# The products of each inner tile in written TensorE order, and another order of the out-projection's products, in two Strassen FFNs on one Trainium2 core

## The chip, the cores and the metric

The kernel runs on one core of one Trainium2 chip. The metric is the device time of one execution in microseconds. The number given for a kernel is the median of its runs. Besides, one execution is recorded by the profiler; its span, from the first to the last instruction, lies a little under its own time, and every row quoted here is of that one execution.

## The reference

The program is one inference step of a streaming encoder with one convolution layer and one attention layer, each followed by a SwiGLU feed-forward network (FFN). 640 tokens (128 of running streams, 512 of a new one) of width 1024 go through it in float32. The change touches the two FFNs alone:

```python
def swiglu_ffn(h, g, w_in, w_out):
    a, b = jnp.split(rms_norm(h, g) @ w_in, 2, axis=-1)
    return h + (jax.nn.silu(a) * b) @ w_out
...
FFN_HIDDEN = -(-8 * D_MODEL // (3 * 256)) * 256
...
    for l in range(DEPTH):
        ...
        h = swiglu_ffn(h, norm_ffn[l], w_ffn_in[l], w_ffn_out[l])
    return rms_norm(h, norm_final), jnp.stack(new_hist, axis=0), k, v
```

The hidden width is 2816, which is 22 tiles of 128.

## The kernel before, in words

**Arithmetic.** A float32 matmul is made of three: each operand is cut into a high part (ScalarE copies it to fp32r, L371) and a low part (VectorE subtracts the high one, L372), and TensorE multiplies high by high, low weights by high tokens, and high weights by low tokens. `put` and `cut` do the cutting, `product` (L432) the three matmuls for each of four blocks of 128 along the contraction: 12 matmuls of 128x320 to one product.

**The FFN.** `ffn` (L333) works through the 22 inner tiles. For each tile the in-projection gives the two halves (a and b) over the two halves of 320 tokens. The first three tiles (`std`, L462) are computed in eight plain block products. The next 19 (`seven`, L524) take a Strassen-like form with seven products of weight sums and token sums. The products are named X11, X21, XT2, XT1, XT3, XT4 and X22 after the token block that they read. X11, XT2, XT3 and XT4 add up in one PSUM tile (`pa`). ScalarE copies `pa` away at three points (`keep`, L451: t1 after X11, t2 after XT2, t3 after XT3), since the next product adds on top of it. A product that goes on in `pa` must wait for the copy ahead of it. X21 stands in a tile of its own (`pb`); XT1 and X22 share a third (`pe`). The last two products, XT4 and X22, are not issued with their tile: `seven` returns a function `after`, and the tile behind it calls this as `before(0)` (XT4) and `before(1)` (X22).

**Weights.** `w_seven` (L410) brings one tile's weights: one 1 MB transfer issued on SyncE's queue (L414) into one of two `raw` buffers, two of 256 KB on GpSimd's into a buffer `s1` that sums two of the blocks, three additions on VectorE (L422, L423, L425) and seven cuts into a ring of 11 slots. A `raw` buffer is free once its last cut has been made, and the next transfer into it is issued then.

**The out-projection.** Tiles come in chunks of six (the first chunk has the three plain ones and three of `seven`). After each chunk `out_chunk` (L555) multiplies its hidden tiles by the output weights, in the same seven-product form for four groups u of output tiles. Its order is the string `QORD` (L65): `52` is product 5 of group 2, a `'` means its first two contraction blocks and a `"` the third alone, so that the work on the first four tiles goes ahead of that on the last two. `a0` and `a1` are the two left-over products of the chunk's last tile. Each finished output product is added to `h` on VectorE (L580).

**What sets the order.** A scheduler places the instructions of the program on each engine by a simulated timeline. `high_priority` lets a piece ahead, `issue_after` and `behind` put a piece after a given instruction. In `out_chunk` each product is issued after the one ahead of it in `QORD`. In `seven` nothing but the data ties the products: the scheduler places their matmuls.

In FFN 0 the `seven` tiles run from 284 to 640 us, in FFN 1 from 1066 to 1421 us. The second repeats the first 782.10 us later almost row by row.

Of the kernel before, what the change touches and what calls it, by code (L numbers as in the profile page):

```python
# [60 lines left out]
NH = NT // 2  # L61
X11, X21, XT2, XT1, XT3, XT4, X22 = range(7)
NCH, CW = 3, 6
HIX = {X11: 0, X21: 1, XT1: 2, XT2: 3, XT3: 4, X22: 5, XT4: 6}
QORD = """50' a0 a1 10' 50" 10" 20 60' 30' 51' 51" 11' 60" 30" 11" 21 70 61 31 40 52 71 12 22 41 62 32 53 72  # L65
          13 23 42 63 33"""
BO = "a0 s0 a1 s1 b0 b1 t0 n0 p0 c0 d0 t1 n1 c1 d1"
BL = "a0 o2 s0 a1 o2 s1 q2 t0 q2 n0 b0 q2 b1 q2 c0 q2 d0 t1 q2 n1 o2 c1 o2 d1 p0 o2"
# [14 lines left out]
def tile_trunk(ctx, tc, xT, vecs, hist, w_pw1, w_pw2, w_in0, w_out0, w_os0, w_in1, w_out1, w_os1,  # L83
               w_kq, w_v, w_o, rel, kc, vc, y_out, convp_out, convs_out, k_out, v_out):
    nc = tc.nc
# [19 lines left out]
    def mmt(n=512):  # L105
        return mm.tile([P, n], F32, tag="mm", name=nm("mm"))
# [4 lines left out]
    h = cst.tile([P, KT, NT], F32, name="h", tag="h")  # L111
# [24 lines left out]
    @contextmanager  # L136
    def behind(*ins):
        with ExitStack() as st:
            for i in ins:
                st.enter_context(tc.issue_after(i))  # L140
            yield
# [191 lines left out]
    def ffn(l, w_in, w_out, w_os, tail, hf, lead=(), b0=None, last_sum=()):  # L333
# [28 lines left out]
        sub, add, mult = ALU.subtract, ALU.add, ALU.mult  # L362
# [47 lines left out]
        def w_seven(src, out=False, first=(), rest=()):  # L410
            n = src.shape[-1] // 4
            raw, ws = wraw(), {}
            s1 = wx.tile([P, 512], F32, tag="s1", name=nm("s1"))[:, :n]
            nc.sync.dma_start(raw[:, :4 * n], src)  # L414
            a12, a11, a21, a22 = (raw[:, n * i:n * i + n] for i in range(4))
            with tc.high_priority(offset=HP), behind(*ties()):
                nc.gpsimd.dma_start(s1, src[:, 2 * n:3 * n])  # L417
                nc.gpsimd.dma_start(s1, src[:, 3 * n:4 * n], accum_op=add)
                for x in ((XT1, X11, X21, XT2, X22, XT3, XT4) if out else
                          (X11, X21, XT2, XT1, XT3, XT4, X22)):  # L420
                    if x == XT2:
                        nc.vector.tensor_tensor(out=a21, in0=a11, in1=a21, op=add)  # L422
                        nc.vector.tensor_tensor(out=a11, in0=s1, in1=a11, op=add)  # L423
                    elif x == X22:
                        nc.vector.tensor_tensor(out=a12, in0=a12, in1=a11, op=add)  # L425
                    ws[x] = slot()
                    with behind(*(first if x == XT1 else rest)):
                        cut(*ws[x], {XT1: s1, X11: a11, X21: a12, XT2: a11, X22: a12, XT3: a21,
                                     XT4: a22}[x])
            return ws  # L430

        def product(pt, w, xs, first, ks=None):  # L432
            (hi, lo), o0 = w
            n = len(xs)
            for k in ks or range(n):
                xh, xl = xs[k]
                c = slice(o0 + k * P, o0 + k * P + P)
                for i, (wt, v) in enumerate(((hi[:, c], xh), (lo[:, c], xh), (hi[:, c], xl))):
                    last = nc.tensor.matmul(pt, wt, v, start=(first and k == i == 0),  # L439
                                            stop=(k == n - 1 and i == 2), skip_group_check=True)  # L440
            return last

        def xproduct(pt, w, x, first):
            return product(pt, w, [(XH[x][:, k, :], XL[x][:, k, :]) for k in range(4)], first)
# [3 lines left out]
        def keep(tag, pt):  # L448
            t = tp.tile([P, NH], F32, tag=tag, name=nm(tag))
            with tc.high_priority(offset=HP):  # L450
                keeps.append(nc.scalar.activation(out=t, in_=pt, func=AF.Copy).ins)  # L451
            return t

        def plus(t, pt):
            with tc.high_priority(offset=HP):
                nc.vector.tensor_tensor(out=t, in0=pt, in1=t, op=add)

        def silu(t, src):
            with tc.high_priority(offset=HP):
                nc.scalar.activation(out=t, in_=src, func=AF.Silu)  # L460
# [27 lines left out]
        def combined(HH, HL, kp, second, held, neg, early=None):  # L488
# [32 lines left out]
                        own(XT4, b21)  # L521
            return sink

        def seven(src, sink, before):  # L524
            ws = w_seven(src)
            pa, pb = mmt()[:, :NH], mmt()[:, :NH]
            xproduct(pa, ws[X11], X11, True)
            t1 = keep("t1", pa)
            before(0)
            xproduct(pb, ws[X21], X21, True)  # L530
            plus(t1, pb)
            silu(t1, t1)
            before(1)
            xproduct(pa, ws[XT2], XT2, False)
            t2 = keep("t2", pa)
            pe = mmt()[:, :NH]
            xproduct(pe, ws[XT1], XT1, True)
            xproduct(pa, ws[XT3], XT3, False)
            t3 = keep("t3", pa)
            plus(t3, pe)  # L540

            def after(i):
                if i == 0:
                    last = xproduct(pa, ws[XT4], XT4, False)
                    sink(0, t1, pa)
                else:
                    last = xproduct(pe, ws[X22], X22, False)
                    plus(t2, pe)
                    silu(t2, t2)
                    sink(1, t2, t3)  # L550
                return last

            return after

        def out_chunk(c, HH, HL, after):  # L555
            ws, pts = {}, {}
            prod = {5: ("e", XT1, True, 1, 1), 1: ("a", X11, True, 0, 0),
                    2: ("b", X21, True, 0, 0), 6: ("a", XT2, False, 1, 0),
                    3: ("e", X22, False, 1, 0), 7: ("a", XT3, False, 1, 1),
                    4: ("a", XT4, False, 0, 1)}  # L560

            def go(i, u, part):
                if u not in ws:
                    o = (4 * c + u) * 12 * P
                    ws[u] = w_seven(w_os[:, o:o + 12 * P], True,
                                    (keeps[2:3], keeps[-2:-1])[u] if c == 0 and u < 2 else (),
                                    keeps[-1:] if (c, u) == (0, 1) else ())
                b, x, first, half, row = prod[i]
                if first and part != '"':
                    pts[b, u] = mmt()[:, :NH]  # L570
                pt = pts[b, u]
                with tc.issue_after(last[0]) if last else nullcontext():
                    ins = product(pt, ws[u][x], list(zip(HH[x], HL[x])), first,
                                  {"": None, "'": (0, 1), '"': (2,)}[part])
                last[:] = [ins.ins]
                if part == "'":
                    return
                hv = h[:, 2 * u + row, half * NH:half * NH + NH]
                with tc.high_priority(offset=HP):
                    nc.vector.tensor_tensor(out=hv, in0=hv, in1=pt, op=sub if row else add)  # L580

            last = []
            for t in QORD.split():
                if t[0] == "a":
                    with tc.issue_after(last[0]):
                        last[:] = [after(int(t[1])).ins]
                else:
                    go(int(t[0]), int(t[1]), t[2:])
            return lambda i: go((7, 4)[i], 3, "")

        def stats(half):
# [77 lines left out]
        for c in range(NCH):  # L669
            for jj in range(NSTD if c == 0 else 0, CW):  # L670
                if jj % 2 == 0:
                    held = [None] * 3
                if jj == NSTD and c == 0:
                    held = helds[1]
                after = seven(w_in[CW * c + jj], combined(HH, HL, jj // 2, jj % 2, held, True),
                              after)
            after = out_chunk(c, HH, HL, after)
            HH, HL = {}, {}
        hids = [(two(2 * jj), two(2 * jj + 1)) for jj in range(FT - NCH * CW)]
        for jj, hid in enumerate(hids):  # L680
            after = seven(w_in[NCH * CW + jj], plain(hid), after)
# [420 lines left out]
    for _ in ffn(0, w_in0, w_out0, w_os0, GR, hf, last_sum=last_sum)[1]:  # L1102
        pass
# [314 lines left out]
    for p in range(NP):  # L1418
# [7 lines left out]
        ha, sa, pt, ps = {}, {}, {}, {}  # L1426
        for op in (BL if p == NP - 1 else BO).split():
            i = int(op[1])
# [34 lines left out]
    with tc.high_priority(offset=HP):  # L1463
        sqs = xp.tile([P, KT, 384], F32, tag="xl1", name=nm("sqs")).rearrange("p a n -> p (a n)")
        acc, r = sqs[:, KT * NH:(KT + 1) * NH], sqs[:, (KT + 1) * NH:(KT + 1) * NH + 8]
        for k in range(KT):
            sq = square(h[:, k, 0:NH], NH, "a", sqs[:, k * NH:(k + 1) * NH])
            if k:
                sq_end = nc.vector.tensor_tensor(out=acc, in0=acc if k > 1 else sqs[:, 0:NH],
                                                 in1=sq, op=ALU.add).ins  # L1470
# [16 lines left out]
    for i in range(SPREAD_AT, KT):  # L1487
        with tc.issue_after(end):
# [4 lines left out]

    hf = ExitStack()
    spare, products = ffn(1, w_in1, w_out1, w_os1, ((256, 384), (0, 256)), hf,
                                     [(split_end[0], i) for i in (adds[1], adds[3], adds[5], sq_end)] +
                                     [(eps_end,)] * 2,
# [73 lines left out]
    last = [next(products) for _ in range(KT)][-1:]  # L1571
# [116 lines left out]
```

## Time and profile before

| | |
|---|---|
| median of 3 runs | 1460.97 us |
| lowest and highest run | 1460.22 and 1462.96 us |
| the profiled execution's own time | 1461.67 us |
| its span | 1459.5 us |
| granted TensorE clock in it | 0.999 |
| TensorE busy | 1432.7 us, 98% of the span |
| VectorE busy | 1144.6 us, 78% |
| ScalarE busy | 758.5 us, 52% |
| GpSimd busy | 297.5 us, 20% |
| moved by DMA | 192.56 MB, 132 GB/s on average |

Times of rows are counted from the start of the span. In a row of the timeline stand the start, the duration, the engine, the line, the operation, output and inputs, and in brackets how long the engine was idle before it and what released it. The matmuls overlap each other, so a busy TensorE is not one that has nothing to wait for: the distance from one start to the next is what counts.

### The profile page before, as it was taken

To read this page: it belongs to the slowest core of one execution; us is meant where nothing else is said; L and a number is where in the kernel's file an instruction comes from. 1 tells how busy PE (TensorE), PEld (TensorE's weight loads), DVE (VectorE), ACT (ScalarE), POOL (GpSimd) and SP (SyncE) were. 2 spreads that over 40 slices of the span, in tenths; PEclk is the share of its full clock that TensorE was granted. 3 is DMA by queue.
4 is the path that set the end of the run, shared out by engine and by line. 5 is a ranking of instruction groups with operands and counts; after the bars stand their busy time and mean duration, and the time that the engine had idled before them with its cause. 6 is when DMAs were issued, how large, how long until landed. Compare 5 with 4: busy or idle time off the path is not lost. (4 is left out here: it accounts for less than half of the span.)

```text
span 1459.5 us, 28220 instructions
## 1 busy us (share of the span) xinstructions
PE 1432.7 (98%) x11022; PEld 1369.1 (94%) x11022; DVE 1144.6 (78%) x2520; ACT 758.5 (52%) x1628; POOL 297.5 (20%) x349
## 2 busy tenths in 40 slices
PE   9999999999999999999999999999999999999998
PEld 8998799999999999999987898878999999999998
DVE  6789867988888888756768668577889788879855
ACT  4666554654554554545564355443554464555443
POOL 5699130011111111013222121011001111111101
PEclk9999999999999999999999999999999999999999
DMA  7267434044534444425556554452134543534522
GB/s 243 74 182 187 121 87 145 14 134 150 138 103 140 141 104 121 116 87 194 181 163 214 179 190 159 140 197 72 39 82 128 151 134 89 175 101 106 162 62 72
DMA packets 66932, 192.56 MB, mean 132 GB/s; under 512 B 12144, under 2 KB 30320, under 8 KB 58480
## 3 DMA queue, kind: packets, MB, share of 16 engines
q1 hardware_dynamic: 52432, 160.58, 33.5%
q0 software_dynamic: 13504, 29.37, 10.0%
q8 instruction: 86, 1.41, 0.4%
q10 hardware_dynamic: 864, 0.83, 0.2%
q14 instruction: 46, 0.38, 0.1%
HBM read 179.14 MB, written 11.61 MB: 131 GB/s over the span
## 5 line engine op out<-in xcount | busy, mean ns | idle before, releaser
L439 PE MATMUL mm<-XH,whi 128*128 128x320 f32 x896 | 276.4, 310 | 4.6 <-ACT t L451 4.2
L439 PE MATMUL mm<-XH,wlo 128*128 128x320 f32 x896 | 276.1, 309 | 0.0
L439 PE MATMUL mm<-XL,whi 128*128 128x320 f32 x896 | 273.9, 309 | 0.0
L371 ACT ACTIVATE whi<-raw 128x512 fp32r<-128x512 f32 (+2 forms) x280 | 168.5, 613 | 134.7 <-PE mm L439 113.5
L372 DVE TENSOR_TENSOR wlo<-raw,whi 128x512 fp32r<-128x512 f32 (+2 forms) x280 | 184.3, 667 | 23.4 <-ACT whi L371 21.6
L199 PE MATMUL mm<-xh,whi 128*128 128x320 f32 (+2 forms) x640 | 200.2, 314 | 1.1 <-ACT whi L164 0.8
L200 PE MATMUL mm<-xh,wlo 128*128 128x320 f32 (+2 forms) x640 | 198.2, 311 | 0.0
L201 PE MATMUL mm<-xl,whi 128*128 128x320 f32 (+2 forms) x640 | 195.9, 311 | 0.4 <-DVE xl L189 0.4
L439 PE MATMUL mm<-hid,whi 128*128 128x320 f32 x732 | 171.8, 310 | 2.7 <-DVE h L580 2.7
L439 PEld LDWEIGHTS mm<-XH,whi 128*128 128x128 f32 x896 | 167.8, 188 | 7.0 <-ACT t L451 6.3
L439 PEld LDWEIGHTS mm<-XH,wlo 128*128 128x128 f32 x896 | 168.2, 188 | 0.0
L439 PEld LDWEIGHTS mm<-XL,whi 128*128 128x128 f32 x896 | 167.6, 188 | 0.0
L439 PEld LDWEIGHTS mm<-hid,whi 128*128 128x128 f32 x732 | 125.1, 188 | 4.3 <-DVE h L580 4.3
L199 PEld LDWEIGHTS mm<-xh,whi 128*128 128x128 f32 x640 | 120.5, 188 | 4.4 <-ACT xh L187 1.5
L201 PEld LDWEIGHTS mm<-xl,whi 128*128 128x128 f32 x640 | 119.7, 188 | 1.2 <-DVE xl L189 0.8
L200 PEld LDWEIGHTS mm<-xh,wlo 128*128 128x128 f32 x640 | 120.5, 189 | 0.2
L439 PE MATMUL mm<-hid,wlo 128*128 128x320 f32 x366 | 113.0, 309 | 0.0
L439 PE MATMUL mm<-XH,shi 128*128 128x320 f32 x344 | 106.0, 309 | 1.1 <-ACT t L451 1.1
L439 PE MATMUL mm<-XH,slo 128*128 128x320 f32 x344 | 106.0, 308 | 0.0
L439 PE MATMUL mm<-XL,shi 128*128 128x320 f32 x344 | 105.6, 308 | 0.0
L841 POOL TENSOR_TENSOR ca<-ca,cvt 128x512 f32<-128x512 f32 x60 | 91.9, 1531 | 17.8 <-ACT cvt L838 11.2
L417 POOL DMA_DIRECT2D s<-in_w_in x38 | 22.1, 582 | 355.7 <-DVE wlo L372 142.2
(275 smaller groups left out, 3372.7 us busy)
## 6 DMA issues: line engine op xcount, KB each, us to landing
raw<-in_w_in SPq DMA_DIRECT2D x38, 1024.0 KB
s<-in_w_in POOLq DMA_DIRECT2D x76, 256.0 KB, 4.2
raw<-in_w_os SPq DMA_DIRECT2D x24, 768.0 KB
cache<-in_ck SPq DMA_DIRECT2D x32, 512.0 KB
cache<-in_cv SPq DMA_DIRECT2D x32, 512.0 KB
raw<-in_w_pw SPq DMA_DIRECT2D x11, 1024.0 KB
s<-in_w_os POOLq DMA_DIRECT2D x48, 192.0 KB, 3.7
raw<-in_w_kq SPq DMA_DIRECT2D x8, 1024.0 KB
```

Of the source, the lines that this page charges most:

```text
L199: nc.tensor.matmul(ps, wh, xh, start=(first and i == 0), stop=False)
L200: nc.tensor.matmul(ps, wl, xh, start=False, stop=False)
L201: end = nc.tensor.matmul(ps, wh, xl, start=False, stop=(stop and i == last))
L371: put_end[1] = nc.scalar.activation(out=hi, in_=src, func=AF.Copy).ins
L372: put_end[0] = nc.vector.tensor_tensor(out=lo, in0=src, in1=hi.bitcast(F32), op=sub).ins
L417: nc.gpsimd.dma_start(s1, src[:, 2 * n:3 * n])
L439: last = nc.tensor.matmul(pt, wt, v, start=(first and k == i == 0), stop=(k == n - 1 and i == 2), skip_group_check=True)
L841: nc.gpsimd.tensor_tensor(out=acc, in0=acc, in1=pr, op=ALU.add)
```

## The change

`seven` gets a list `row` that holds the last matmul of the product that was issued last, and a helper `following` that issues each product behind it. So the seven products of a tile, with the two left over from the tile ahead in their written places, stand on TensorE one after the other: X11, XT4 of the tile ahead, X21, X22 of the tile ahead, XT2, XT1, XT3. `out_chunk` begins behind the same instruction. The name `row` for the sign of an output product becomes `low` there, and lines move by two behind L524 and by nine behind L564. `QORD` takes another order in its second third: `60"`, `30"` and `70` come earlier, `51"` and `11` (now in one piece) and `40` too.

```diff
-QORD = """50' a0 a1 10' 50" 10" 20 60' 30' 51' 51" 11' 60" 30" 11" 21 70 61 31 40 52 71 12 22 41 62 32 53 72
+QORD = """50' a0 a1 10' 50" 10" 20 60' 30' 51' 60" 30" 51" 70 11 21 40 61 31 52 71 12 22 41 62 32 53 72
           13 23 42 63 33"""
...
+        row = []
+
         def seven(src, sink, before):
             ws = w_seven(src)
             pa, pb = mmt()[:, :NH], mmt()[:, :NH]
-            xproduct(pa, ws[X11], X11, True)
+
+            def following(f, *args):
+                with behind(*row):
+                    last = f(*args)
+                if last is not None:
+                    row[:] = [last.ins]
+
+            following(xproduct, pa, ws[X11], X11, True)
             t1 = keep("t1", pa)
-            before(0)
-            xproduct(pb, ws[X21], X21, True)
+            following(before, 0)
+            following(xproduct, pb, ws[X21], X21, True)
             plus(t1, pb)
             silu(t1, t1)
-            before(1)
-            xproduct(pa, ws[XT2], XT2, False)
+            following(before, 1)
+            following(xproduct, pa, ws[XT2], XT2, False)
             t2 = keep("t2", pa)
             pe = mmt()[:, :NH]
-            xproduct(pe, ws[XT1], XT1, True)
-            xproduct(pa, ws[XT3], XT3, False)
+            following(xproduct, pe, ws[XT1], XT1, True)
+            following(xproduct, pa, ws[XT3], XT3, False)
             t3 = keep("t3", pa)
             plus(t3, pe)
...
-                hv = h[:, 2 * u + row, half * NH:half * NH + NH]
+                hv = h[:, 2 * u + low, half * NH:half * NH + NH]
                 with tc.high_priority(offset=HP):
-                    nc.vector.tensor_tensor(out=hv, in0=hv, in1=pt, op=sub if row else add)
+                    nc.vector.tensor_tensor(out=hv, in0=hv, in1=pt, op=sub if low else add)
+                return ins
 
-            last = []
+            last = row[:]
```

Only TensorE, ScalarE and VectorE get another order, and only in the parts of both FFNs from their first `seven` tile on. The numbers of instructions stay, but for a few that do no work.

**TensorE where `seven` begins in FFN 0** (from 284 us on in the trace before). In the names, `mm_399_3438` is `pa` and `mm_403_3482` is `pe` of the first `seven` tile, `mm_400_3439` its `pb`, and `mm_407_3532` is `pa` of the second tile. XH0 to XH3 are the high tokens of X11, X21, XT2 and XT1. Left out are matmuls that go on in the same product. Before:

```order
L439 MATMUL mm_399_3438<-XH0_317_2811,shi_325_2834 128x320 [waits Activation_49]
L439 MATMUL mm_400_3439<-XH1_319_2813,shi_327_2836 128x320 [waits Activation_49]
L439 MATMUL mm_400_3439<-XH1_319_2813,slo_328_2837 128x320 [waits DVE_49]
L439 MATMUL mm_403_3482<-XH3_307_2801,whi_321_2830 128x320 [waits DVE_49,Activation_49]
L439 MATMUL mm_407_3532<-XH0_317_2811,whi_323_2832 128x320 [waits Activation_49]
L439 MATMUL mm_399_3438<-XH0_317_2811,slo_326_2835 128x320 [waits DVE_49]
L439 MATMUL mm_408_3533<-XH1_319_2813,whi_323_2832 128x320 [waits DVE_49]
L439 MATMUL mm_399_3438<-XH2_309_2803,shi_329_2838 128x320 [waits Activation_49]
```

After:

```order
L439 MATMUL mm_399_3438<-XH0_317_2811,shi_325_2834 128x320 [waits Activation_49]
L439 MATMUL mm_399_3438<-XH0_317_2811,slo_326_2835 128x320 [waits DVE_49]
L439 MATMUL mm_400_3439<-XH1_319_2813,shi_327_2836 128x320 [waits Activation_49]
L439 MATMUL mm_399_3438<-XH2_309_2803,shi_329_2838 128x320 [waits Activation_49]
L439 MATMUL mm_399_3438<-XH2_309_2803,slo_330_2839 128x320 [waits DVE_49]
L439 MATMUL mm_403_3482<-XH3_307_2801,whi_321_2830 128x320
L439 MATMUL mm_399_3438<-XH4_311_2805,whi_321_2830 128x320 [waits Activation_49]
L439 MATMUL mm_407_3532<-XH0_317_2811,whi_323_2832 128x320
```

Before, XT2 (the first matmul with XH2) stands 60 matmuls behind the first one of X11, with the X11 and X21 products of the second tile ahead of it; now it stands 24 behind.

**ScalarE at the second `seven` tile of FFN 0** (297 to 302 us in the trace before). `t3_404_3507` is the first tile's keep t3, `t1_409_3546` the second tile's keep t1, and `raw_415_3647` the third tile's weights. Before:

```order
L451 ACTIVATE t2_402_3480<-mm_399_3438 128x320 [waits PE_49]
L371 ACTIVATE shi_329_2838<-raw_405_3510 128x512 [waits DVE_49,Activation_49]
L371 ACTIVATE hid_383_3331<-B00_354_2976 128x320 [waits DVE_49]
L451 ACTIVATE t1_409_3546<-mm_407_3532 128x320 [waits DVE_49]
L371 ACTIVATE hid_389_3345<-B01_366_3109 128x320 [waits DVE_49]
L451 ACTIVATE t3_404_3507<-mm_399_3438 128x320 [waits PE_49]
L371 ACTIVATE whi_323_2832<-s1_430_3781 128x384 [waits DMASW7_49]
L371 ACTIVATE hid_377_3272<-hid_343_2852 128x320 [waits DVE_49]
L460 ACTIVATE t1_409_3546<-t1_409_3546 128x320 [waits DVE_49]
L451 ACTIVATE t2_412_3617<-mm_407_3532 128x320 [waits PE_49]
L371 ACTIVATE whi_321_2830<-raw_415_3647 128x512 [waits DMAHW5_49]
```

After:

```order
L451 ACTIVATE t2_402_3480<-mm_399_3438 128x320 [waits PE_49]
L371 ACTIVATE shi_329_2838<-raw_405_3510 128x512 [waits Activation_49]
L371 ACTIVATE hid_389_3345<-B01_366_3109 128x320 [waits DVE_49]
L371 ACTIVATE hid_377_3272<-hid_343_2852 128x320 [waits DVE_49]
L371 ACTIVATE whi_321_2830<-raw_415_3647 128x512 [waits DMAHW5_49,PE_49]
L451 ACTIVATE t3_404_3507<-mm_399_3438 128x320 [waits PE_49]
L371 ACTIVATE whi_321_2830<-raw_415_3647 128x512
L451 ACTIVATE t1_409_3546<-mm_407_3532 128x320 [waits PE_49]
```

The keep t3 of the first tile has changed places with the first cut of the third tile's weights, which waits for a DMA.

**VectorE near the end of the first chunk's out-projection** (343 to 351 us in the trace before). `raw_461_4193` is the weight buffer of the next tile, `raw_456_4098` that of the last group of output weights; `mm_454_4046` is the PSUM tile of group 2 in which products 12, 62 and 72 add up; its addition to `h` must have read it before the next of them goes on. `mm_455_4057` is that of 22, and `mm_449` that of 11, 61, 71 and 41. Before:

```order
L580 TENSOR_TENSOR h_73<-h_73,mm_455_4057 128x320 [waits DVE_49,PE_49]
L372 TENSOR_TENSOR wlo_322_2831<-raw_456_4098,whi_321_2830 128x384 [waits Activation_49]
L372 TENSOR_TENSOR slo_330_2839<-raw_456_4098,shi_329_2838 128x384 [waits Activation_49]
L580 TENSOR_TENSOR h_73<-h_73,mm_449_3933 128x320 [waits PE_49]
L372 TENSOR_TENSOR slo_328_2837<-raw_456_4098,shi_327_2836 128x384 [waits Activation_49]
L422 TENSOR_TENSOR raw_461_4193<-raw_461_4193 128x512 [waits DMAHW2_49]
L580 TENSOR_TENSOR h_73<-h_73,mm_454_4046 128x320 [waits PE_49]
```

After:

```order
L589 TENSOR_TENSOR h_73<-h_73,mm_449_3951 128x320 [waits PE_49]
L372 TENSOR_TENSOR slo_326_2835<-raw_456_4098,shi_325_2834 128x384 [waits Activation_49]
L422 TENSOR_TENSOR raw_461_4193<-raw_461_4193 128x512 [waits DMAHW2_49]
L425 TENSOR_TENSOR raw_456_4098<-raw_456_4098 128x384 [waits DVE_49]
L589 TENSOR_TENSOR h_73<-h_73,mm_454_4046 128x320 [waits PE_49]
L372 TENSOR_TENSOR wlo_322_2831<-raw_456_4098,whi_321_2830 128x384 [waits Activation_49]
L589 TENSOR_TENSOR h_73<-h_73,mm_455_4057 128x320 [waits DVE_49,PE_49]
```

The addition that waits for the next tile's DMA (L422) has moved up ten rows, from behind the additions to `h` of products 12, 22 and 41 to ahead of them.

More of the change, by code (lines that the diff above doesn't have):

```diff
@@ L567, in go @@
                                     keeps[-1:] if (c, u) == (0, 1) else ())
-                b, x, first, half, row = prod[i]
+                b, x, first, half, low = prod[i]
                 if first and part != '"':
```

## Prediction

> **What bounds the kernel.** I read the busy shares first, then the waits of TensorE, then the places of those waits in the timeline.
>
> ```profile
> PE 1432.7 (98%) x11022; PEld 1369.1 (94%) x11022; DVE 1144.6 (78%) x2520; ACT 758.5 (52%) x1628; POOL 297.5 (20%) x349
> 355.00:430.00 75.00, 75.00 (x514) 75.00 (x513) 63.54 (x122) 43.16 (x88) 9.99 (x14) 1.00 0.44 121
> PE mm L439 <- ACT t L451: 5.3, 10, 1.0
> PE mm L439 <- DVE h L580: 5.2, 9, 1.0
> ```
>
> TensorE sets the end. In the middle of a chunk (second row: busy time and instructions of PE, weight loads, VectorE, ScalarE and GpSimd, then clock, DMA share and GB/s) VectorE has 63.54 of 75 us to do, so it can be late only after a burst. The two last rows are what TensorE waits for in the FFNs: ten times the copy of a sum (keep, L451), nine times the addition of an output product to h. So an order that waits nowhere can win 10.5 us of 1459.5, under 1%; one wait of 4 us takes back as much as four of those 1.0 us.
>
> **Gain: the keeps.** One of the ten, at 296 us:
>
> ```profile
> 296.24 0.31 PE L439 MATMUL mm<-XL,shi 128*128 128x320 f32 x1
> 296.59 0.44 ACT L451 ACTIVATE t<-mm 128x320 f32<-128x320 f32 x1 [4.85 <-PE mm L439]
> 297.08 0.41 PE L439 MATMUL mm<-XH,whi 128*128 128x320 f32 x1 [0.53 <-ACT t L451]
> 297.33 0.31 PE L439 MATMUL mm<-XH,wlo 128*128 128x320 f32 x1
> 301.73 0.31 PE L439 MATMUL mm<-XH,wlo 128*128 128x320 f32 x1
> ```
>
> From 297.33 to 301.73 lie 30 steps, so a matmul takes 4.40/30 = 0.147 us. From the last matmul of XT2 to the first of XT3 it is 0.84 us, as XT3 stands directly behind and waits for the copy: 0.69 us lost, and 0.10 more as the next start follows after 0.25 instead of 0.147. In the new order 12 matmuls of XT1, 1.76 us, lie between XT2 and XT3, and six of output product 5 or twelve of X11 between XT3 and XT4. The chain of 0.84 us fits in either, over an idle ScalarE. Eight of the ten waits go, some 0.8 us each: **-6.4 us**. The two at the FFNs' very ends stay, as XT4 there has only two matmuls of other work ahead of it. Bounds: 0 if ScalarE is always late by another step, -10.5 if all waits of both kinds went.
>
> **Cost A: the first tile of seven in each FFN.** The new order asks for XT2 after 24 matmuls, the old one after 60. Who makes the low weights of XT2?
>
> ```profile
> 284.07 0.45 PE L439 MATMUL mm<-XH,shi 128*128 128x320 f32 x2
> 289.73 0.68 DVE L425 TENSOR_TENSOR raw<-raw 128x512 f32<-128x512 f32 x1
> 290.33 0.68 DVE L372 TENSOR_TENSOR slo<-raw,shi 128x512 fp32r<-128x512 f32 x1
> 290.94 0.48 DVE L372 TENSOR_TENSOR hid<-B,hid 128x320 fp32r<-128x320 f32 x1
> 291.34 0.68 DVE L372 TENSOR_TENSOR slo<-raw,shi 128x512 fp32r<-128x512 f32 x1
> 1066.17 0.46 PE L439 MATMUL mm<-XH,shi 128*128 128x320 f32 x2
> 1073.42 0.68 DVE L372 TENSOR_TENSOR slo<-raw,shi 128x512 fp32r<-128x512 f32 x1
> 284.00:296.00 12.00, 12.00 (x84) 12.00 (x83) 11.43 (x23) 5.22 (x11) 2.93 (x4) 1.00 0.40 78
> ```
>
> The row at 291.34 writes XT2's low weights, done at 292.02. It is the 390th VectorE instruction in both orders, and VectorE works without a break up to it (11.43 of 12 us): it comes no sooner. TensorE now wants it with the 26th matmul from 284.07 on, at 284.07 + 25 x 0.1467 = 287.74. It waits 292.02 - 287.74 = 4.3 and 0.1 for the restart, **4.4 us**. In FFN 1: 1074.10 - 1069.84 = 4.3, also **4.4**. Before, products of the second tile filled this time; they are not lost, but they don't cover any longer. Below it could fall only if VectorE had less to do ahead of row 390, and the pieces that move there are one of each kind in for one out, 0.6 us: 3.7 to 5.0.
>
> **Cost B: the second tile.** XT4 of the first tile waits for keep t3. In the new ScalarE order that keep stands directly behind the first cut of the third tile's weights, which waits for a transfer.
>
> ```profile
> 293.55 0.68 DVE L372 TENSOR_TENSOR wlo<-raw,whi 128x512 fp32r<-128x512 f32 x1
> 294.25 0.33 SPq L414 DMA_DIRECT2D raw<-in_w_in  x1
> 299.14 0.44 ACT L451 ACTIVATE t<-mm 128x320 f32<-128x320 f32 x1 [0.55 <-PE mm L439]
> 301.74 2.19 ACT L371 ACTIVATE whi<-raw 128x512 fp32r<-128x512 f32 x4 [0.41 <-DMA raw<-in_w_in]
> 480.51 0.33 SPq L414 DMA_DIRECT2D raw<-in_w_in  x1
> 485.37 0.69 DVE L422 TENSOR_TENSOR raw<-raw 128x512 f32<-128x512 f32 x1 [0.50 <-DMA raw<-in_w_in]
> ```
>
> The transfer is issued when the raw buffer's last cut ends (293.55 + 0.68 = 294.23, row 294.25), and ScalarE takes it at 301.74, 7.5 us on. The keep (299.14) went ahead of it before. In the new order VectorE makes that last cut one instruction later (0.40), so the data land at about 302.1; the cut takes 0.53 (the four of the group 2.19) and the keep 0.44. XT4 can go on at 303.1. TensorE reaches it 72 matmuls behind 284.07 (X11, X21, XT2, XT1, XT3 and the second tile's X11) and A's 4.4 us late, at 284.07 + 10.56 + 4.4 = 299.0. It waits 4.1, with the restart **4.2 us** in each FFN. Lower bound: a transfer as short as the one at 480.51 (485.37 - 480.51 = 4.9 us) lands at 299.5 and costs 1.5. Queued behind the cut are also the next keep and the cuts of the third tile; the latter are wanted a tile later, some 10 us.
>
> **Cost D: the chunks' output products.** The old order lets the addition L422, which waits for the next tile's transfer, stand ahead of the addition to h for which product 72 waits:
>
> ```profile
> 451.71 0.46 PE L439 MATMUL mm<-hid,whi 128*128 128x320 f32 x2
> 458.31 0.46 PE L439 MATMUL mm<-hid,whi 128*128 128x320 f32 x2
> 462.42 0.69 DVE L422 TENSOR_TENSOR raw<-raw 128x512 f32<-128x512 f32 x1 [2.34 <-DMA raw<-in_w_in]
> 463.03 0.48 DVE L580 TENSOR_TENSOR h<-h,mm 128x320 f32<-128x320 f32 x1
> 463.56 0.41 PE L439 MATMUL mm<-hid,shi 128*128 128x320 f32 x1 [0.99 <-DVE h L580]
> 327.29 0.42 PE L439 MATMUL mm<-hid,shi 128*128 128x320 f32 x1 [0.57 <-DVE h L580]
> ```
>
> Now L422 and L425 stand ahead of 12's addition, so 62 waits for it, and 62 stands 27 matmuls (3.96 us) ahead of 72. The transfer can't come as much sooner: it is released by product 40 (its last matmul in the 451.71 row), which moves ahead by only 18 matmuls, 2.64 us, and by a VectorE queue shorter by 0.8. In the second chunk: landing 462.42 - 3.44 = 459.0, then 0.61, 0.47 and 0.48 for the two additions and that to h: 460.5, against 62 at 458.45 (second of the 458.31 pair): 2.1 us instead of 1.24 before. By the same working the first chunk gets 0.8 for 0.6. Taken over six chunks, 0.7 each: **+4 us** (0 if the transfer lands 2 us sooner, 12.6 if each is 2.1 us late with no old wait to set against it).
> Earlier in the chunk 60" now comes 9 matmuls (1.32 us) sooner and 70 only six behind it. The wait at 327.29 is of this kind: the low parts of the chunk's last hidden tile are late. I put **+2.4 us** for both FFNs, 0.4 a chunk; 0 if the cuts come sooner with the written order, 6 x 1.32 = 7.9 if all of the 1.32 us becomes a wait.
>
> **Sum.** 2 x 4.4 + 2 x 4.2 - 6.4 + 4 + 2.4 = +17.2 us. Against the profiled execution's own 1461.67 this is 1478.9. That lies 0.7 above the median of 1460.97, so I say **1478 us**.
>
> The waits of A and B are longer than any TensorE wait in the FFNs before (1.0), and matmuls were slow once, at the start of the program:
>
> ```profile
> 2.00:6.00 4.00, 4.00 (x20) 4.00 (x20) 1.07 (x3) 1.51 (x2) 0.49 (x2) 1.00 0.97 329
> 7.00:9.00 2.00, 2.00 (x19) 2.00 (x19) 1.90 (x5) 0.85 (x2) 0.00 (x0) 1.00 0.98 339
> ```
>
> The first row has 20 matmuls in 4 us, 200 ns each, the second 19 in 2, 105 ns, though the clock column reads 1.00 in both: TensorE begins at half speed for some 4 us.
>
> **Rivals.** (1) *The transfer of B lands before keep t3 is wanted, or the keep is held only shortly.* For it: landing took 4.9 us at 480.51. Against: it took 7.5 here in the same traffic. B falls to 1.5 or less, and with D halved: 1478 - 5.4 - 3.2 = 1469. (2) *TensorE falls to the half speed of its start after each of the four waits.* For it: the rows above. Against: it is shown only for the start of the program; no wait inside the FFNs before reaches beyond 1.0. With 4 us at half speed behind each wait, 2 us of work lost each: 4 x 2 = 8, so 1486. The Trainium skill, "TensorE: Matmul & The Clock Gate", section "Part 1: The HAM clock gate (the "warmup" mystery)", has the clock halved after about one idle window of 3.4 us, and says that the window runs freely. An estimate by that page: a wait of 4.3 us covers a whole window in about a quarter of cases ((4.3 - 3.4) / 3.4), which makes 2 us of the 8 and a time of 1480; no row here can show it. (3) *The delay is earned back.* While TensorE waits 8 us in each FFN, VectorE and the transfers run ahead, and the waits of D shrink away. Against: each transfer is released by TensorE's own progress (two raw buffers), so a lead is kept for two tiles at most. D 0, old waits on h of 5.2 gone: 1478 - 6.4 - 5.2 = 1466. (4) *Faster: the start isn't held by VectorE.* If the rows ahead of 390 close up by 4 us once TensorE frees their slots in another order, A is 0, B by its lower bound 1.5 each, and D 0: 1461 + 3 - 6.4 = 1458. It decides where A, B and D come to less than 6.4 us in all. Against: 11.43 busy of 12 us leaves 0.6 to close up, not 4. (5) *The order isn't the written one.* The listing of the instructions shows it is.
>
> **Chances.** Forecast 0.60; (1) 0.13; (2) 0.08; (3) 0.12; (4) with what lies between it and no change, 0.07. The likeliest case by its own bounds (A 3.7 to 5.0, B 3 to 5, D 2 to 12) goes from 1461 + 13.4 - 6.4 + 2 = 1470 to 1461 + 20 - 6.4 + 12 = 1487. With (1) and most of (3) below it, the range is **1465 to 1487**. No change that can be measured here is within 0.2%, 2.9 us; that takes A to D at 3.5 to 9.3 us in all, 0.03; faster by more 0.04; slower 0.93.
>
> **What would show it.** A: in the changed trace a wait of about 4.3 us on VectorE's slo at 288 and at 1070 with the wait's end at 292.0. B: a wait of about 4 us on the keep near 299, ScalarE's cut of raw directly ahead of it, idle on a DMA. Gain: no wait on L451 between products inside the chunks. D: waits on the addition to h at 62 and 60" in place of 72. The forecast is wrong if VectorE's row 390 ends much before 292, if the third tile's transfer lands before 299, or if the waits are there and the time isn't.

## The result, and the profile after

| | before | after |
|---|---|---|
| median | 1461.97 us (4 runs, 1460.22 to 1464.0) | 1483.41 us (4 runs, 1481.02 to 1486.89) |
| the profiled execution's own time | 1461.67 us | 1481.02 us |
| its span | 1459.5 us | 1478.9 us |
| granted TensorE clock in it | 0.999 | 0.997 |

The runs before are the three given ahead and one more. The changed kernel takes 1.0139 times as long, with a 95% interval of 1.0121 to 1.0156. The page's busy shares after:

```profile
PE 1438.2 (97%) x11022; PEld 1371.2 (93%) x11022; DVE 1148.0 (78%) x2520; ACT 758.9 (51%) x1628; POOL 297.3 (20%) x349
```

The view of TensorE's waits after (total, times, longest):

```profile
PE mm L439 <- ACT t L451: 7.9, 6, 2.3
PE mm L439 <- DVE h L589: 5.6, 9, 0.9
PE mm L439 <- DVE slo L372: 4.6, 2, 2.3
PE mm L439 <- ACT shi L371: 3.2, 2, 1.6
PE mm L439 <- DVE hid L372: 3.0, 6, 0.5
```

The number of instructions and the work of the other engines are as before. The waits of TensorE in the FFNs were 5.3 + 5.2 = 10.5 us and are now 24.3. The waits on keeps (L451) are fewer, but longer: 10 of at most 1.0 us have become 6 of at most 2.3. Three kinds are new: the low and the high part of a weight sum (slo, shi), twice each, and the low part of a hidden tile (hid), six times.

**The start of the seven-product tiles.** The timeline of TensorE and VectorE in FFN 0, after:

```profile
283.62 0.31 PE L439 MATMUL mm<-XH,shi 128*128 128x320 f32 x1
288.89 0.41 PE L439 MATMUL mm<-XH,shi 128*128 128x320 f32 x1 [1.60 <-ACT shi L371]
290.88 0.68 DVE L372 TENSOR_TENSOR slo<-raw,shi 128x512 fp32r<-128x512 f32 x1
291.62 0.63 PE L439 MATMUL mm<-XH,slo 128*128 128x320 f32 x1 [2.31 <-DVE slo L372]
292.05 0.47 PE L439 MATMUL mm<-XL,shi 128*128 128x320 f32 x1
292.32 0.47 PE L439 MATMUL mm<-XH,shi 128*128 128x320 f32 x1
294.45 0.40 PE L439 MATMUL mm<-XL,shi 128*128 128x320 f32 x1
```

Two stretches of the windows view there, TensorE alone (its busy time and matmuls, the granted clock, DMA share, GB/s):

```profile
291.60:294.60 3.00, 2.98 (x11) 0.50 0.72 101
295.00:298.00 3.00, 3.00 (x22) 1.00 0.84 230
```

XT2 begins at 288.89 instead of 287.14, since the copy of its high part is late too, and then waits for the low part, written from 290.88 to 291.56. Both waits together are 4.33 us. Behind them matmuls start 0.267 us apart (292.05, 292.32). The windows say why: 11 matmuls in 3 us at a granted clock of 0.50, against 22 at 1.00 right behind.

**The keep behind a transfer**, the timeline of ScalarE and TensorE at the second tile:

```profile
301.30 0.63 ACT L371 ACTIVATE whi<-raw 128x512 fp32r<-128x512 f32 x1 [4.74 <-DMA raw<-in_w_in]
301.83 0.42 ACT L451 ACTIVATE t<-mm 128x320 f32<-128x320 f32 x1
302.31 0.42 PE L439 MATMUL mm<-XH,whi 128*128 128x320 f32 x1 [2.18 <-ACT t L451]
```

The cut waits 4.74 us for its data, the keep stands behind it, and XT4 waits for the keep.

**The turn from one chunk to the next**, the timeline of VectorE and TensorE:

```profile
366.41 0.42 PE L439 MATMUL mm<-hid,whi 128*128 128x320 f32 x1 [0.44 <-DVE h L589]
369.24 0.69 DVE L422 TENSOR_TENSOR raw<-raw 128x512 f32<-128x512 f32 x1 [0.68 <-DMA raw<-in_w_in]
369.85 0.48 DVE L589 TENSOR_TENSOR h<-h,mm 128x320 f32<-128x320 f32 x1
370.38 0.41 PE L439 MATMUL mm<-hid,whi 128*128 128x320 f32 x1 [0.63 <-DVE h L589]
```

The row at 366.41 is product 73, that at 370.38 is 43: these are the two that `out_chunk` leaves to the next chunk's first tile. 43 waits for the addition to h of 73, and that stands on VectorE behind L422, which waits for a transfer.

**The low part of the last hidden tile**, in the same view:

```profile
335.81 0.88 DVE L372 TENSOR_TENSOR hid<-B,hid 128x320 fp32r<-128x320 f32 x2
336.35 0.41 PE L439 MATMUL mm<-hid,shi 128*128 128x320 f32 x1 [0.50 <-DVE hid L372]
```

This is product 60". It waits 0.66 us in each of the six chunks and costs 0.94 with two restarts and a further short wait at 70.

In the table below a wait counts as what the distance between two starts has over 0.147 us, with the slower restart behind it; that is some tenths more than the idle time in the rows.

| in the profiled execution | before | after | difference |
|---|---|---|---|
| XT2 of the first tile, waits | - | 4.33 + 4.32 | +8.7 |
| slow steps behind it | - | 1.45 + 1.60 | +3.0 |
| keep t3 of the first tile, ahead of XT4 | - | 2.45 + 2.57 | +5.0 |
| the eight keeps that the change aims at | 6.8 | - | -6.8 |
| other keeps (513.60, 527.73 and 1205.58) | - | 0.29 + 1.82 + 1.63 | +3.7 |
| 60" and what follows at 70 | | 5.6 | |
| 62, 73 and 43 at the turn | | 9.8 | |
| output products in all | 8.3 | 15.4 | +7.1 |
| sum | | | +20.7 |

The own times differ by 19.35; the seven-product tiles began 0.45 us earlier (283.62 against 284.07). Where the other 0.9 us went was not traced.

### The profile page after: what moved, and what is told of

The parts are those of the page before. It is cut to its first block, busy times and chain, and to the rows that moved or that the text cites. A ratio compares the mean times of both kernels' runs of the same rounds, so it can differ in the third digit from the quotient of the medians.

```text
span 1478.9 us, 28238 instructions
## 1 busy us (share of the span) xinstructions
PE 1438.2 (97%) x11022; PEld 1371.2 (93%) x11022; DVE 1148.0 (78%) x2520; ACT 758.9 (51%) x1628; POOL 297.3 (20%) x349
## 5 line engine op out<-in xcount | busy, mean ns | idle before, releaser
L422 DVE TENSOR_TENSOR raw<-raw 128x512 f32<-128x512 f32 (+1 forms) x62 | 39.7, 640 | 73.3 <-DMA raw<-in_w_in 59.0
```

## The experiments

**chain_only**: the change with the former QORD.

```diff
-QORD = """50' a0 a1 10' 50" 10" 20 60' 30' 51' 60" 30" 51" 70 11 21 40 61 31 52 71 12 22 41 62 32 53 72
+QORD = """50' a0 a1 10' 50" 10" 20 60' 30' 51' 51" 11' 60" 30" 11" 21 70 61 31 40 52 71 12 22 41 62 32 53 72
```

> The change with the former QORD put back, so the chain of products alone. In the trace of the change the chain's own waits are 11.7 us at the two first tiles of seven (XT2), 5.0 us at the two second tiles (keep t3), 3.7 us on two later keeps and 9.9 us at the chunks' turns (73 and 43), and six waits of 0.94 us on the low parts of the last hidden tile (product 60") belong to the new QORD. Theory: the chain carries nearly all of it, so 1478 to 1483 us, with the waits at XT2, keep t3, 73 and 43 in place and the six waits at 60" gone. Rival: the new QORD carries half or more of the loss: 1472 us or less.

Measured: 1472.31 us (1467.98 to 1477.47), 1.0068 of before [1.0046, 1.0091]. The theory missed, and the time all but met the rival's 1472: the chain alone carries just under half of the loss. (The next run shows that the new QORD doesn't carry the other half alone.) The profiled execution was the slowest of the six, 1477.47 us. In it the waits at XT2 were there unchanged (4.34 and 4.33 us), and those at 60" and the long ones at 73 and 43 were gone (at most 0.5 us was left). In their place 72 waited for its addition behind L422, as in the kernel before. Its waits, and the longest one in the timeline:

```profile
PE mm L439 <- DVE h L589: 6.6, 6, 2.2
PE mm L439 <- ACT t L451: 5.0, 6, 2.0
```

```profile
583.70 0.69 DVE L422 TENSOR_TENSOR raw<-raw 128x512 f32<-128x512 f32 x1 [3.54 <-DMA raw<-in_w_in]
584.31 0.48 DVE L589 TENSOR_TENSOR h<-h,mm 128x320 f32<-128x320 f32 x1
584.85 0.42 PE L439 MATMUL mm<-hid,whi 128*128 128x320 f32 x1 [2.19 <-DVE h L589]
```

**qord_only**: the kernel before with the new QORD alone (the same lines the other way round).

> The kernel before with the new QORD alone. Theory: the products of the in-projection stay where the scheduler put them, so no wait at XT2 of the first tile and none at 73 and 43; what comes is at most six waits of 0.94 us at 60", against 3 to 5 us of old waits that go: 1460 to 1466 us. Rival (the order of the output products moves the transfer behind which the additions to h queue): 1468 us or more.

Measured: 1460.14 us (1459.15 to 1463.21), 0.9985 [0.9974, 0.9995]. The theory held. In its waits those at 60" came (the first row), and others on h went from 5.2 to 2.5:

```profile
PE mm L439 <- DVE hid L372: 4.2, 6, 1.0
PE mm L439 <- ACT t L451: 2.6, 6, 0.5
PE mm L439 <- DVE h L580: 2.5, 5, 0.6
```

So the parts don't add up: +0.68% and -0.15% make +1.39% together. The new QORD wins a little where the scheduler may place 73 and 43 freely, and loses where the chain holds them in their written places. The next run tests the second half of this; the former QORD with 73 and 43 free was not run.

**free_turn**: the chain without 73 and 43. `tiles[0]`, here and below, counts the tiles of seven in an FFN from 1; tiles 4, 10 and 16 begin behind a chunk. The lines that do the counting are left out.

```diff
-            following(before, 0)
+            (following if tiles[0] not in (4, 10, 16) else lambda f, i: f(i))(before, 0)
...
-            following(before, 1)
+            (following if tiles[0] not in (4, 10, 16) else lambda f, i: f(i))(before, 1)
```

> The change, with the two left-over output products of each chunk (73 and 43) left out of the chain; the rest stays chained. Theory: in the changed kernel 73 stands nine matmuls behind 63 and 43 twelve behind 73, and their additions to h stand on VectorE behind cuts or behind L422, which waits for a transfer; with 24 and 18 matmuls between them the waits of 9.9 us over six chunks go: 1483.4 - 9.9 = 1473.5 us. Rival (VectorE is late there whatever stands between, so the next product waits instead): less than 3 us are won, 1480 us or more.

Measured: 1472.8 us (1471.96 to 1474.25), 1.0069 [1.0054, 1.0084]. The theory held: 10.6 us won. The waits at 73 were gone in all six chunks, those at 43 were 0.3 to 1.1 us in five. On TensorE 24 matmuls now stood between 63 and 73. That it equals the time of chain_only agrees with the place: either part of the change without the other leaves 73 and 43 all but free of waits.

**free_start**: the chain begins with the third tile.

```diff
-                with behind(*row):
+                with behind(*(row if tiles[0] > 2 else ())):
```

> The change, with the first two tiles of seven of each FFN left out of the chain (it begins with the third). Theory: the waits at XT2 (5.8 and 5.9 us with the slow matmuls behind them) and at the keep t3 ahead of XT4 (2.5 and 2.6) go, one wait of 0.8 us on a keep in each FFN comes back: 1483.4 - 16.8 + 1.6 = 1468 us, and every later wait stays. Rival (the delay is only moved: VectorE and the transfers lose the lead that the waits gave them): later waits grow and the time stays above 1475 us.

Measured: 1469.54 us (1467.47 to 1474.17), 1.0039 [1.0022, 1.0056]. By the medians the theory held within 1.5 us. In the timeline the start shows only the keep wait of the kernel before:

```profile
297.24 0.41 PE L439 MATMUL mm<-XH,whi 128*128 128x320 f32 x1 [0.53 <-ACT t L451]
```

But the later waits did not all stay as they were. In the profiled execution (1472.75 us, 3.2 above the median) the waits behind the first two tiles come to 26.9 us in both FFNs, against 20.2 in the changed kernel. Most of the 6.7 us is at product 10" of the first chunk, which waited 1.4 and 2.9 us for hidden low parts and in the changed kernel not at all. The longer one:

```profile
1111.15 0.56 DVE L422 TENSOR_TENSOR raw<-raw 128x384 f32<-128x384 f32 x1 [1.42 <-DMA raw<-in_w_os]
1112.09 0.49 DVE L372 TENSOR_TENSOR hid<-B,hid 128x320 fp32r<-128x320 f32 x1
1112.63 0.41 PE L439 MATMUL mm<-hid,whi 128*128 128x320 f32 x1 [2.64 <-DVE hid L372]
```

The low part stands on VectorE behind an addition that waits for output weights. In the changed kernel the same addition finds its data landed:

```profile
1118.86 0.56 DVE L422 TENSOR_TENSOR raw<-raw 128x384 f32<-128x384 f32 x1
```

So a part of the delay at the start is earned back later, as the rival says, though far less than the rival asks for.

**keep_ahead**: the third tile's cuts behind the first tile's keep t3.

```diff
-            ws = w_seven(src)
+            t3 = keeps[-4:-3] if tiles[0] == 3 else ()
+            ws = w_seven(src, False, t3, t3)
```

> The change, with the cuts of each FFN's third tile of seven put behind the keep t3 of its first tile, so that this keep doesn't stand behind a cut that waits for a transfer. Theory: the waits ahead of XT4 (2.5 and 2.6 us) go, the cuts lose 0.4 us of no account: 1483.4 - 5 = 1478.4 us, with the wait at XT2 unchanged. Rival (the tile is late for another reason, such as X21 of the second tile or the weights of the third): the wait reappears within a tile and the time stays within 1 us.

Measured: 1480.82 us (1477.65 to 1482.25), 1.0120 [1.0104, 1.0136]. In the timeline the keep no longer waits for the cut, and the cut still waits for its data:

```profile
299.04 0.44 ACT L451 ACTIVATE t<-mm 128x320 f32<-128x320 f32 x1 [1.84 <-PE mm L439]
301.93 1.15 ACT L371 ACTIVATE whi<-raw 128x512 fp32r<-128x512 f32 x2 [2.45 <-DMA raw<-in_w_in]
310.48 0.41 PE L439 MATMUL mm<-XH,shi 128*128 128x320 f32 x1 [0.92 <-ACT t L451]
```

XT4 went through, but the second tile's XT3 waited at 310.48, 1.2 us (0.4 in FFN 1). Of 5.0 us, 3.5 were won in the trace. The medians differ by 2.6, but the intervals of the two kernels overlap. The rows show the order on ScalarE as the cause of this wait, and that a part of it passed to the next keep.

**warm_gap** and **warm_gap24**: 12 or 24 wasted matmuls in each FFN's first tile between X21 and XT2. XT1 starts its tile anew, so nothing of them gets into the result.

```diff
             following(before, 1)
+            if tiles[0] == 1:
+                pe = mmt()[:, :NH]
+                following(xproduct, pe, ws[X11], X11, True)
+                following(xproduct, pe, ws[X21], X21, True)
             following(xproduct, pa, ws[XT2], XT2, False)
...
-            pe = mmt()[:, :NH]
+            if tiles[0] > 1:
+                pe = mmt()[:, :NH]
```

(warm_gap has the first of the two products alone.)

> The change, with 12 wasted matmuls (one more X11 product into the tile of XT1, which XT1 overwrites) in each FFN's first tile of seven between X21 and XT2, where TensorE waits 4.3 us. In the trace of the change the ten to twelve matmuls behind that wait start 0.267 us apart instead of 0.147. Theory: TensorE slows down because it stood still for over 4 us; with the 12 matmuls it stands still 2.6 us at a stretch, the matmuls behind come 0.147 us apart and the end of the wait doesn't move: 1.4 us less in each FFN, 1480.5 us. Rival (the slow steps have to do with the weights or with VectorE's writes at that time): they stay 0.267 us apart and the time doesn't change.

Measured: 1483.71 us (1482.0 to 1488.02), 1.0143 [1.0118, 1.0168]: no gain. Behind a wait now under 2 us, seven matmuls came 0.147 us apart, and then 13 came 0.26. The timeline, and windows of half a microsecond:

```profile
292.22 0.41 PE L439 MATMUL mm<-XH,slo 128*128 128x320 f32 x1 [1.70 <-DVE slo L372]
293.36 0.34 PE L439 MATMUL mm<-XL,shi 128*128 128x320 f32 x1
293.50 0.46 PE L439 MATMUL mm<-XH,shi 128*128 128x320 f32 x1
293.76 0.47 PE L439 MATMUL mm<-XH,slo 128*128 128x320 f32 x1
```

```profile
292.50:293.00 0.50, 0.50 (x5) 1.00 0.00 0
293.50:294.00 0.50, 0.50 (x4) 0.50 0.76 111
296.50:297.00 0.50, 0.50 (x4) 0.59 0.92 136
297.00:297.50 0.50, 0.50 (x5) 1.00 0.39 98
```

In FFN 1 the same wait was followed by no slow steps. The clock fell from 293.50 on for 3.4 us, though TensorE had been busy again for 1.3 us. That no time was won has a further reason: XT4's waits for the keep were still there, 2.36 us at 303.11 and 3.40 at 1093.42, and slow steps now stood behind both. The FFNs had four such stretches of 3.4 us in this execution, against two in the changed kernel. Neither the theory (a wait of over 4 us is needed) nor its rival says that; the last section takes it up.

> As warm_gap, with 24 wasted matmuls (products X11 and X21 into the tile that XT1 overwrites) in place of 12, so that TensorE stands still for under 1 us of the 4.3. With 12, still standing 2 us, it was slow behind one of the two waits (14 steps of 0.267 us) and not behind the other (2). Theory (the slow steps come from standing still): in both FFNs the matmuls behind XT2's first two come 0.147 us apart, and the end of XT2's wait stays where it was: 1.2 to 2.9 us less in each FFN, 1479 to 1481 us. Rival (they come from something else at that place): 10 or more slow steps in at least one FFN.

Measured: 1476.09 us (1472.79 to 1478.81), 1.0095 [1.0073, 1.0117]. With TensorE busy throughout there were no slow steps at this place in either FFN, as the theory said. It was 3 us faster than expected. One reason lies in the order: with the wasted matmuls in its timeline the scheduler put keep t3 ahead of the cut of raw again, and the wait ahead of XT4 was gone too. The slow steps had to do with standing still, then. The same kernel shows them at another place, behind a 1.9 us wait at 331.39.

**mid_chain**: free_start and free_turn together.

> The change, with both the first two tiles of seven and 73 and 43 left out of the chain. Theory: the two savings add up, since the waits lie in different places: free_start's 1469.5 less the 10.9 us that its trace shows at 73 and 43, 1459 us, a little under the kernel before. Rival (they share a cause, VectorE's backlog, and one replaces the other): 1464 us or more.

Measured: 1461.43 us (1457.93 to 1463.46, 10 runs), 0.9984 [0.9973, 0.9996]. The two savings add up nearly: 2.4 us are missing. Product 10" of the first chunk waited 2.1 and 1.8 us, which it does not in free_turn, and waits of 2.9 us stayed at 43, in five turns. With both places free, nothing is left of the loss, and nothing is won either: qord_only, without any chain, has the same ratio (0.9985).

**qord_mid**: the kernel before, no chain, a third order.

```diff
+QORD = """50' a0 a1 10' 50" 10" 20 60' 30' 51' 11' 60" 30" 51" 70 11" 21 40 61 31 52 71 12 22 41 62 32 53 72
           13 23 42 63 33"""
```

> The kernel before with a third order of the output products: as the new QORD, but with the first part of 11 (six matmuls, 0.88 us) ahead of 60", and its last part behind 70. Theory: the six waits of 0.75 to 1.3 us on the low parts of the last hidden tile at 60" shrink by 0.7 us each: 1460.1 - 4 = 1456 us. Rival (the early sum of 11 takes a PSUM tile, or VectorE is late by more): 1460 us or more.

Measured: 1458.37 us (1456.69 to 1459.31), 0.9968 [0.9955, 0.9981]. The time lies between the theory's 1456 and the rival's 1460. It beats the kernel before, by 0.3%, and the changed one. The waits at 60" shrank to 0.4 us or none; the first chunks got one of 1.8 us at 40, which keeps back part of the gain.

**mid_both**: mid_chain with the order of qord_mid.

> mid_chain (the change without the chain in the first two tiles of seven and without 73 and 43 in it) with the order of output products of qord_mid. Theory: the two gains add up; mid_chain's six waits of 0.64 to 0.76 us at 60" and six of 0.2 behind it shrink by 0.5 us each, 3 us: 1461.4 - 3 = 1458 us, no better than qord_mid alone (1458.4), since the chain's remaining gain at the keeps (two waits of 0.8 in place of four) is given back at 10" of the first chunk (2.1 and 1.8 us). Rival (the chain in the middle of the chunks is worth what the keeps cost): 1455 us or less.

Measured: 1464.80 us (12 runs, 1462.36 to 1466.3), 1.0018 [1.0007, 1.0028]. Both readings fell: with the other QORD the chain cost 0.5% again (1.0018 against 0.9968). The trace shows four waits of 1.1 to 1.4 us and several shorter ones on keeps, in and near the turns. The first of the four, on VectorE, ScalarE and TensorE:

```profile
365.79 0.69 DVE L422 TENSOR_TENSOR raw<-raw 128x512 f32<-128x512 f32 x1 [1.76 <-DMA raw<-in_w_in]
368.12 0.47 ACT L460 ACTIVATE t<-t 128x320 f32<-128x320 f32 x1 [3.85 <-DVE t L456]
369.01 0.42 ACT L451 ACTIVATE t<-mm 128x320 f32<-128x320 f32 x1
369.49 0.41 PE L439 MATMUL mm<-XH,whi 128*128 128x320 f32 x1 [1.11 <-ACT t L451]
```

The keep stands behind a silu, that behind an addition on VectorE, and that behind L422, which waits for a transfer; two more of the four (595.93 and 1264.36) look the same. Why the transfers come too late with this order isn't settled.

## Why the prediction was right, step by step

**Slower, by about this much.** 1478 us was forecast, a loss of 17.2; the medians differ by 21.4, the profiled executions by 19.4. The two large causes stood where the prediction put them, and taking them away (free_start) took 13.9 us of the 21.4. That the sum came so close is partly luck: B was 3.4 us too large, and the slow steps (3.0) and three new waits on keeps (3.7) were not in it.

**Cost A: right, and one part missing.** A wait of 4.3 us was worked out from VectorE's row 390; 4.33 and 4.32 were measured, with the row's end at 291.56 for 292.02 (all began 0.45 earlier). In the traces of both kernels it is the 456th VectorE instruction, so it did keep its place. That the first 1.76 us of it were waits on the high part changes nothing in the sum. What was mis-sized is the restart: 0.1 in the sum, 1.45 and 1.60 in the trace. This is the second rival's mechanism, which the forecast left out of the sum. It came behind the two longest waits and not behind all four, and cost 3.0 us instead of 8.

**Cost B: right mechanism, too large.** 4.2 was forecast, 2.45 and 2.57 measured, below the prediction's own bounds of 3 to 5. Two terms of it were off. The data landed at 301.30, not 302.1, since the transfer was issued at 294.20 (with everything else 0.45 us earlier than worked out) and took 7.1 us instead of 7.5; and TensorE, slowed down, reached XT4 only at 299.97, not at 299.0. The rows of keep_ahead show the cause.

**Gain: right size, but not kept.** The eight waits on keeps went, 6.8 us for 6.4. The step that failed is "the chain of 0.84 us fits in either, over an idle ScalarE". Three keeps stood behind instructions that were late. The longest, at 527.73 (1.8 us), stood behind two silu, those behind VectorE's additions, and these behind L422:

```profile
523.36 0.69 DVE L422 TENSOR_TENSOR raw<-raw 128x512 f32<-128x512 f32 x1 [2.53 <-DMA raw<-in_w_in]
525.48 0.47 ACT L460 ACTIVATE t<-t 128x320 f32<-128x320 f32 x1 [0.53 <-DVE t L456]
526.88 0.47 ACT L460 ACTIVATE t<-t 128x320 f32<-128x320 f32 x1 [0.41 <-DVE t L456]
527.73 0.42 PE L439 MATMUL mm<-XH,shi 128*128 128x320 f32 x1 [1.55 <-ACT t L451]
```

**Cost D: wrong place, and the right size by luck.** +6.4 was forecast, +7.1 measured. But the wait that was worked out, 62 behind L422, was 0.15 to 0.35 us in four chunks and none in the other two: the transfer landed early enough. 4 us had been put on it. 8.8 us came at 73 and 43 instead, which the prediction didn't look at: it followed the new QORD and forgot that the chain also fixes the two products that `out_chunk` leaves behind. The early part (60") was put at 0.4 us a chunk and was 0.94. These errors cancel against the old waits, 8.3 us, that went.

**The rivals.** The transfer of B did not land early (1): it took 7.1 us, and the wait stayed above 1.5. For D it did land early enough for 62, but other products waited instead. Of the delay a part was earned back (3): later waits are 6.7 us longer in the profiled execution of free_start, where TensorE has no such wait at the start. The waits of D did not go, though, as (3) has it. Faster (4) is excluded by the rows of VectorE.

## What to carry to other kernels

A written order on one engine takes from the scheduler the freedom to fill a wait with the next tile's work; here it cost most at the first tile and at the turns, where the weights are still being made. Confined to the places where the data run ahead, it cost nothing with one order of the output products (mid_chain against qord_only) and 0.5% with another (mid_both against qord_mid), and it won nothing: the fastest kernel, qord_mid, has no chain. Beside the engine that is put in order, look at what the others now have in their queues ahead of each thing it waits for: in the changed kernel all waits of over 1 us but those at XT2 came from an instruction that waited for a transfer and had something urgent standing behind it. And two edits measured apart don't tell what they do together: here +0.68% and -0.15% made +1.39%.

## What the runs showed of the hardware

The clock falls in fixed windows. In the twelve profiled executions of this study every change of the granted clock lies on a grid of 3.413 us, and each stretch at 0.50 ahead of the program's end is 3.41 or 6.83 us long (from 291.22 to 294.63 in the changed kernel). I added up TensorE's idle time, in which no matmul's row stands, in each window at full clock from 100 us on; the last fall, which comes in every execution when TensorE's work has ended, is left out. With 1.60 us or less (21 windows with 1.1 to 1.6) the next window was always at full clock; with 1.70 to 3.00 us (14 windows) it was always at half. So it isn't the length of a wait that counts but how much of it falls into one window: the wait of 2.34 us at 302.31 was cut in two by a window's edge (1.33 and 0.84 us idle) and cost nothing more, while the wait at the same place in warm_gap, 2.36 us at 303.11, fell into one window (2.20 us idle), and slow steps followed. The one of 1.96 us at 292.22 in warm_gap also fell into one window and cost 1.6 us, and the fall came 1.3 us after TensorE had gone on. Around 29 us, with other matmuls, windows with 1.19 to 1.23 us idle were followed by half clock in five executions, and windows with 1.20 in four others were not; that isn't explained.

The Trainium skill, "TensorE: Matmul & The Clock Gate", section "Part 1: The HAM clock gate (the "warmup" mystery)", gives 3413 ns for the window and says that it runs freely, and the traces agree. That about one idle window is needed doesn't agree: half a window was enough. A window at half clock costs at most 3.41 / 2 = 1.7 us.

The profiled executions of before and qord_only had no window at half clock ahead of the program's end, that of chain_only five in the FFNs and one at 29 us: its own time is 1477.47 us where the kernel's median is 1472.31. So I expect that the time of a kernel with waits near 1.7 us depends on where the grid lies. How much of the spread between runs this makes was not shown, since only one execution of each kernel has a trace.
